# Start order, position table, order of sums at the first gate product, and one spread of a norm in an encoder layer

## The chip, the cores and the metric

The kernel runs on one core of a Trainium2 chip. The metric is the device time of one execution in microseconds; the time before is the median of three runs, 1468.25 us (1464.38 to 1468.91). Five engines work side by side, each through its own queue: TensorE (PE in the profile, its weight loads PEld), VectorE (DVE), ScalarE (ACT), GpSimd (POOL) and SyncE (SP), which here only issues DMAs. DMAs are issued by SyncE, ScalarE and GpSimd.

## The reference

One layer of an encoder for 256 tokens of width 2048 in float32. The parts that matter here:

```python
h = rms_norm(x, attn_norm[i])
proj = h @ w_in[i]
qa, ka, va, qb, kb, vb, ga, gb = jnp.split(proj, split_points, axis=-1)
ya = windowed_gqa(qa, ka, va, rel_bias_table, sink_a[i])
yb = dilated_attention(qb, kb, vb, rel_bias_table)
merged = jax.nn.sigmoid(ga) * (ya @ w_branch_a[i]) + jax.nn.sigmoid(gb) * (yb @ w_branch_b[i])
x = x + merged @ w_out[i]
hf = rms_norm(x, ffn_norm[i])
g = dwconv_centred(hf @ w_ffn_gate[i], conv_w[i], conv_b[i])
x = x + (jax.nn.gelu(g) * (hf @ w_ffn_up[i])) @ w_ffn_down[i]
gate_p = jax.nn.sigmoid(rms_norm(x, ple_norm[i]) @ w_ple_gate[i])
x = x + gate_p * (p[i] @ w_ple_proj[i])
return rms_norm(x, final_norm)
```

Both attentions add a bias to their logits: `table[t5_bucket(rel)]`, a row of a table of 32 buckets by 20 heads, picked by the distance of the two positions.

## The kernel before

**Products.** Every float32 weight is split into two float32r parts, a high one (`whi`, a ScalarE copy, line 261) and a low one (`wlo`, a VectorE subtraction, line 262); activations are split alike (`halves`, `gained`). A product is then taken from three partial products: high by high, high by low, low by high. The weights lie in device memory in the order of use, in pieces of 16 blocks of 128x128; `load` fetches half a piece (512 KB), `split_to` splits it, and `block` and `wide_product` ask for the split three pieces ahead of use. In `block` (lines 324 and 325) the weight is held and 512 columns stream for the high part, 256 for the low one. In `wide_product` (356 to 358) and `seven_product` (400 to 402) the activation is held and 512 weight columns stream. `seven_product` is used for the output and the down projection and forms a 2x2 block product with seven multiplications; its banks are called p1 to p7 and c22.

**Order.** `_plan` writes the list of jobs: first keys, queries and values, then the gates and branch products in quarters, then `o` (output projection, two halves of the columns, n = 0 and 1), then `gg` (the first two gate products together, 32 blocks), then u, g, u, g and so on to the half, `d0`, the second half of the feed-forward beginning with gate product 22 (job `_HALF`), `d1`, then `pp` and `pg`, the embedding part. Work of the other engines is hung into these jobs by `at((job, block), function, ...)`, which `run_due` calls before that block. The program's scheduler may reorder the instructions of an engine; `keep` holds the instructions given to it in program order among themselves.

**Start.** ScalarE issues the norm's columns `cl` (8 KB) and then the first 128 KB chunk of x; SyncE issues the weights and the other chunks of x in the order of the list `order`. TensorE runs `WARM` products of ones in the meantime (line 213). The first seven products share the moving chunks of x (`hs`, lines 454 and 455) and run block by block as they come; 16 chunks are needed, and the first 16 weight blocks form piece 0. The next half piece is the ninth transfer that SyncE issues.

**Position table.** `oh` (which bucket each distance falls into, 32x512) and `tb` (32x20) are loaded on SyncE after all x; one float32 product (line 584) picks the biases, a mask is added (586), and they go to device memory, from where `bias` reads them back.

**The first gate product.** The output projection ends with `joined`, which adds the banks p2, p3, p4 and c22 to the residual rows (line 905) and squares each sum for the second norm (`squares_of`, line 856). (p2, t=0) and (p4, t=1) form one block of 512 columns, (p3, t=0) and (c22, t=1) the next. `flip` turns two column chunks with eight transposes (866) and scales and splits them by `gained` (454 and 455) into `hf`, the moving operand of the gate products; four flips of the last half run inside `gg`, whose blocks 16 to 31 read them. `rms` hangs in the norm: `ask` sums the squares (468), takes the root (474 on VectorE, 476 on GpSimd) and scales the identity into two diagonals `rdg` (484); `tell` spreads them over all partitions by a product with ones (490) and copies the result (501) into `rt[1]`, which the gate's follow-up `after` multiplies in (768).

Of the kernel before, what the change touches and what calls it, by code (L numbers as in the profile page):

```python
# [10 lines left out]
F32 = mybir.dt.float32  # L11
FR = mybir.dt.float32r
AF = mybir.ActivationFunctionType
ALU = mybir.AluOpType
AX = mybir.AxisListType

P = 128
T = 256
D = 2048
# [8 lines left out]
NH = QH + BH  # L28
NBUCK = 32
# [4 lines left out]
EPS = 1e-6  # L34
# [100 lines left out]
FIRST = 7  # L135
START = FIRST + 1
_JOBS = _plan()
WARM = 9
_HALF = next(i for i, j in enumerate(_JOBS) if j[0] == "g" and j[1] == FHALF)


# [48 lines left out]
def _encoder(ctx: ExitStack, tc, xt, pt, cols, table, onehot, mask, ident_in, last_gain, wts, xrows, out):  # L190
    nc = tc.nc
# [7 lines left out]

    x = const.tile([P, KC, T], F32, name="x")  # L200
    cl = const.tile([P, 4 * KC + 4 * FC + QH], F32, name="cl")
    nc.scalar.dma_start(cl[:, :KC], cols[:, :KC])
    nc.scalar.dma_start(x[:, 0:1, :], xt[:, 0:1, :])
    ident = const.tile([P, P], F32, name="ident")
    ones = const.tile([P, P], F32, name="ones")
    nc.vector.memset(ones, 1.0)
# [16 lines left out]
    keep = tc.keep_in_program_order  # L223
# [5 lines left out]
    held = {}  # L229
# [203 lines left out]
    sc = ctx.enter_context(tc.tile_pool(name="sc", bufs=2))  # L433
# [31 lines left out]
    def rowsums(parts):  # L465

        s = sc.tile([P, 2], F32, name="sum")
        nc.vector.tensor_reduce(s, parts, axis=AX.X, op=ALU.add)
        return s

    def root(s, n):

        v = sc.tile([P, n], F32, name="rv", bufs=3)
        nc.vector.tensor_scalar(v, s, 1.0 / D, EPS, op0=ALU.mult, op1=ALU.add)
        r = sc.tile([P, n], F32, name="rr", bufs=3)
        nc.gpsimd.tensor_tensor(r, v, mhalf[:, :n], op=ALU.pow)
        return r

    def norm(s, n):

        r = root(s, n)
        dg = sc.tile([P, T], F32, name="rdg", bufs=1)
        for t in range(2):
            nc.vector.tensor_scalar(dg[:, t * P:(t + 1) * P], ident, r[:, t:t + 1], None, op0=ALU.mult)
        return r, dg

    def spread(dg):
# [5 lines left out]
    def rms(i, total, key, n):  # L493

        def ask():
            rc[key], dg = norm(total(), n)

            def tell():
                b = spread(dg)
                rt[key] = sc.tile([P, T], F32, name="rms")  # L500
                nc.scalar.activation(rt[key], b, AF.Copy)
            for e in i[1:]:
                at(e, tell)
        at(i[0], ask)
# [4 lines left out]
    def at(i, f, *a):  # L509

        due.setdefault(i, []).append((f, a))
# [7 lines left out]
    ap_ = att.enter_context(tc.tile_pool(name="att", bufs=2))  # L519
# [5 lines left out]
    hb1 = big.tile([P, GRP * AW + BH * BW], F32, name="hb1", tag="b1", bufs=1)  # L525
    hba = [hb0, hb1[:, :GRP * AW].rearrange("p (h n) -> p h n", h=GRP)]
    hbb = hb1[:, GRP * AW:].rearrange("p (h n) -> p h n", h=BH)
    oh = ap_.tile([NBUCK, 2 * T], F32, name="oh", tag="near", bufs=2)
    tb = sc.tile([NBUCK, NH], F32, name="tb", bufs=1)
    mk = ap_.tile([NH, 2 * T], F32, name="mk", tag="s1", bufs=2)  # L530

    order = [(0, 1), (0, 0, 1), (0, 1, 3), (0, 3, SUB), (1, 2), (0, SUB, 12), (0, 12, PIECE), (2, 3)]
    chunk = 3
    for r in range(1, FIRST):
        need = -(-((r + 1) * PIECE) // FIRST)
# [3 lines left out]
    for step in order:  # L539
        if len(step) == 3:  # L540
            load(*step)
        elif step[0]:
            nc.sync.dma_start(x[:, step[0]:step[1], :], xt[:, step[0]:step[1], :])
    nc.sync.dma_start(cl[:, KC:], cols[:, KC:])
    nc.sync.dma_start(ident, ident_in)
    nc.sync.dma_start(oh, onehot)
    nc.sync.dma_start(tb, table)
    nc.sync.dma_start(mk, mask)

# [12 lines left out]
    for step in order:  # L562
# [6 lines left out]
        while state["at"] < min(FIRST * ready, _SUBS[state["sub"]][0]):  # L569
            k, e = divmod(state["at"], FIRST)  # L570
# [9 lines left out]
    split_to(state["sub"] + 2)  # L580


    b = ps.tile([NH, 2 * T], F32, name="misc")
    nc.tensor.matmul(b, tb, oh, start=True, stop=True)
    rows = ap_.tile([NH, 2 * T], F32, name="rows", tag="s1", bufs=2)
    keep(nc.vector.tensor_tensor(rows, b, mk, op=ALU.add))
    hold = dram.tile([NH, 2 * T], F32, name="hold")
# [266 lines left out]
    def squares_of(n, t, parts):  # L854
        r = res[:, t, n * W4:(n + 1) * W4]
        keep(nc.scalar.activation(row(), r, AF.Square, accum_out=parts[:, t, n:n + 1]))
# [45 lines left out]
    def joined(n, t, acc, parts):  # L902

        r = res[:, t, n * W4:(n + 1) * W4]
        nc.vector.tensor_tensor(r, acc, r, op=ALU.add)
        squares_of(n, t, parts)

    def gate(n, t, acc, last):

# [48 lines left out]
    for i, job in enumerate(_JOBS):  # L958
# [44 lines left out]
                nc.scalar.dma_start(pr[k], pt[:, k, :])  # L1003
            at((i + 1, 18), layered, pr)
        if kind == "gg":
            rms([(i, 26), (i + 1, 2), (_HALF, 9)], lambda: rowsums(held["ss1"]), 1, 2)
        if kind in ("ga", "gb"):
            at((i, 6), fetch, int(kind == "gb"), n)
        if kind == "bb":
# [2 lines left out]
        if kind == "o":  # L1012
            if n:
                at((i, 11), features)
            for e, k in enumerate((8, 10, 12, 14) if n else (12, 12, 14, 14)):
                at((i + 1, k), flip, 8 * n + 2 * e, "hf", 1)
        if kind == "d1":
            for e, j in enumerate([(i + 2, 0), (i + 2, 0), (i + 3, 1), (i + 3, 1)] if n else
# [41 lines left out]
        if i == FIRST:  # L1060
            for e in range(FIRST):
                late = max(e - KVH, 0)
                at((START + late, 5 if late else 13), after, _JOBS[e], START, None, firsts[e])
            at((START, 13), after, job, START, acc)
        elif kind == "gg":
            for e in range(2):
                at((i + 1, 4 + 4 * e), after, ("g", e), i, acc[e])
        elif kind in ("ga", "gb", "ba", "bb"):
            if kind == "ga":
                if n < QUARTERS - 1:  # L1070
                    th = ap_.tile([P, 2, 2, W4], F32, name="th", tag="v", bufs=1)
                    held["th", n] = {"ga": [th[:, 0, t] for t in range(2)], "gb": [th[:, 1, t] for t in range(2)]}
                else:
                    th = ap_.tile([P, 2, W4], F32, name="th", tag="s3", bufs=1)
                    held["th", n] = {"ga": [th[:, t] for t in range(2)],
                                     "gb": [ap_.tile([P, W4], F32, name="th", tag="s1", bufs=2) for t in range(2)]}
            if kind == "ba":
                held["m"] = ap_.tile([P, 2, W4], F32, name="m", tag="vf", bufs=1)
            for t in range(2):
                if t:  # L1080
                    rest()
                gated(kind, n, t, acc[t])
        elif kind in ("o", "d0", "d1"):
            parts = held["ss1" if kind == "o" else "ss2"]
            for name, t, c in (("p2", 0, 0), ("p3", 0, 1), ("p4", 1, 0), ("c22", 1, 1)):
                if end:
                    joined(2 * n + c, t, acc[name], parts)
                else:
                    a = row()
                    nc.scalar.activation(a, acc[name], AF.Copy)  # L1090
                    to_residual(n, t, c, a)
                    if kind != "d0":
                        at((i + 1, 10), squares_of, c, t, parts)
        elif kind == "pg":
            for t in range(2):
                if t:
                    rest()
                tail = gate(n, t, acc[t], last)
                if last:
                    finish(t, tail)  # L1100
            if n == QUARTERS - 2:
                so_far()
        else:
            after(job, i, acc)
# [49 lines left out]
```

## Time and profile before

| | |
|---|---|
| time, median of three runs | 1468.25 us (1464.38 to 1468.91) |
| profiled execution: span from first to last instruction | 1463.2 us |
| median less span: what lies around it | 5.05 us |
| HBM read, written | 324.06 MB, 27.30 MB |
| cost of all float32 weight splits, ScalarE and VectorE (lines 261, 262; 556 of each) | 564.2 and 650.7 us |
| most frequent DMA: 512 KB of weights, 477 of them, issue to landing | 5.0 us, median |

The profile is one execution on the chip. The profiled execution's own time outside its span is not recorded; the table sets its span beside the median. A line such as L262 is a line of the kernel. In the timeline a row gives start, length, engine, instruction, its output and inputs, and in brackets the engine's idle time before it and what ended it. Matmuls overlap in the pipeline, so the distance from one start to the next says more of them than the length shown.

### The profile page before, as it was taken

To read this page: it belongs to the slowest core of one execution; us is meant where nothing else is said; L and a number is where in the kernel's file an instruction comes from. 1 tells how busy PE (TensorE), PEld (TensorE's weight loads), DVE (VectorE), ACT (ScalarE), POOL (GpSimd) and SP (SyncE) were. 2 spreads that over 40 slices of the span, in tenths; PEclk is the share of its full clock that TensorE was granted. 3 is DMA by queue.
4 is the path that set the end of the run, shared out by engine and by line. 5 is a ranking of instruction groups with operands and counts; after the bars stand their busy time and mean duration, and the time that the engine had idled before them with its cause. 6 is when DMAs were issued, how large, how long until landed. Compare 5 with 4: busy or idle time off the path is not lost.

```text
span 1463.2 us, 20802 instructions
## 1 busy us (share of the span) xinstructions
PE 1449.4 (99%) x7507; PEld 1234.3 (84%) x7507; DVE 1137.2 (78%) x1653; ACT 832.9 (57%) x1196; POOL 107.3 (7%) x178
## 2 busy tenths in 40 slices
PE   9999999999999999999999999999999999999997
PEld 8888888888888888888888888888888888788886
DVE  7687665665665668889998989897999987988665
ACT  7465444444444456665566655675656555666654
POOL 0000000001111100201111100102110100010000
PEclk9999999999999999999999999999999999999999
DMA  9754555557888967978788786989878864797652
GB/s 322 245 177 159 172 170 171 188 178 262 286 314 294 354 229 254 296 237 283 269 293 270 273 284 212 285 287 304 279 273 282 289 244 159 266 294 249 217 193 89
DMA packets 111731, 362.17 MB, mean 248 GB/s; under 512 B 12804, under 2 KB 17924, under 8 KB 111500
## 3 DMA queue, kind: packets, MB, share of 16 engines
q1 hardware_dynamic: 88908, 292.80, 57.5%
q0 software_dynamic: 20560, 63.71, 14.4%
q10 hardware_dynamic: 2160, 4.33, 0.9%
q8 instruction: 59, 0.97, 0.3%
q14 instruction: 44, 0.36, 0.1%
HBM read 324.06 MB, written 27.30 MB: 240 GB/s over the span
## 4 chain that ended last, share of the span: by engine, by line
PE 96%; DVE 1%; issue 1%; DMA 1%; ACT 0%; POOL 0%; POOLq 0%; DVEq 0%; ACTq 0%
PE acc L324 28%; PE acc L325 14%; PE acc L356 9%; PE acc L358 9%; PE acc L357 9%; PE acc L401 7%; PE acc L400 7%; PE acc L402 7%; PE first L324 2%; PE first L325 1%; PE pt L669 1%; DMA raw<-in_wts 0%; PE pt L866 0%; DVE wlo L262 0%; PE sp L628 0%
## 5 line engine op out<-in xcount | busy, mean ns | idle before, releaser
L262 DVE TENSOR_TENSOR wlo<-raw,whi 128x1024 fp32r<-128x1024 f32 (+2 forms) x556 | 650.7, 1181 | 264.3 <-ACT whi L261 258.9
L261 ACT ACTIVATE whi<-raw 128x1024 fp32r<-128x1024 f32 (+2 forms) x556 | 564.2, 1025 | 473.5 <-PE acc L358 188.7
L324 PE MATMUL acc<-mov,whi 128*128 128x512 f32 x1840 | 642.2, 395 | 0.3 <-DVE mov L455 0.3
L325 PE MATMUL acc<-mov,wlo 128*128 128x256 f32 x1840 | 511.0, 278 | 0.0
L324 PEld LDWEIGHTS acc<-mov,whi 128*128 128x128 f32 x1840 | 345.0, 188 | 79.5 <-DVE mov L455 0.6
L325 PEld LDWEIGHTS acc<-mov,wlo 128*128 128x128 f32 x1840 | 346.0, 188 | 0.5
L356 PE MATMUL acc<-whi,mov 128*128 128x512 f32 (+1 forms) x512 | 196.5, 384 | 0.0
L358 PE MATMUL acc<-whi,mov 128*128 128x512 f32 (+1 forms) x512 | 196.3, 383 | 0.0
L357 PE MATMUL acc<-wlo,mov 128*128 128x512 f32 (+1 forms) x512 | 196.2, 383 | 0.0
L356 PEld LDWEIGHTS acc<-whi,mov 128*128 128x128 f32 x512 | 96.7, 189 | 19.3 <-DVE first L444 0.8
L358 PEld LDWEIGHTS acc<-whi,mov 128*128 128x128 f32 x512 | 96.6, 189 | 18.8
L357 PEld LDWEIGHTS acc<-wlo,mov 128*128 128x128 f32 x512 | 96.6, 189 | 18.4
L400 PE MATMUL acc<-whi,act 128*128 128x512 f32 x207 | 80.9, 392 | 0.2 <-ACT whi L261 0.2
L401 PE MATMUL acc<-wlo,act 128*128 128x512 f32 x207 | 80.9, 391 | 0.0
L402 PE MATMUL acc<-whi,act 128*128 128x512 f32 x207 | 80.6, 389 | 0.0
L825 POOL DMA_DIRECT2D x<-row x36 | 31.1, 879 | 380.0 <-ACT row L830 258.1
L262 DVE TENSOR_TENSOR wlo<-sums,whi 128x1024 fp32r<-128x1024 f32 x37 | 45.1, 1219 | 9.9 <-ACT whi L261 9.9
L400 PEld LDWEIGHTS acc<-whi,act 128*128 128x128 f32 x207 | 38.8, 188 | 9.5 <-ACT whi L261 1.5
L401 PEld LDWEIGHTS acc<-wlo,act 128*128 128x128 f32 x207 | 38.9, 188 | 8.9 <-DVE wlo L262 0.9
L401 PE MATMUL acc<-wlo,shl 128*128 128x512 f32 x116 | 45.6, 393 | 0.0
L402 PEld LDWEIGHTS acc<-whi,act 128*128 128x128 f32 x207 | 38.9, 188 | 8.0
L402 PE MATMUL acc<-whi,shl 128*128 128x512 f32 x116 | 45.2, 390 | 0.0
(203 smaller groups left out, 1669.5 us busy)
## 6 DMA issues: line engine op xcount, KB each, us to landing
raw<-in_wts SPq DMA_DIRECT2D x477, 512.0 KB, 5.0
sums<-kept SPq DMA_DIRECT2D x37, 512.0 KB, 5.6
sums<-in_wts POOLq DMA_DIRECT2D x23, 512.0 KB, 6.8
kept<-sums POOLq DMA_DIRECT2D x23, 512.0 KB, 4.1
raw<-in_wts SPq DMA_DIRECT2D x39, 256.0 KB, 4.9
row<-in_wts POOLq DMA_DIRECT2D x37, 256.0 KB, 8.2
x<-row POOLq DMA_DIRECT2D x36, 256.0 KB, 7.7
two<-in_wts POOLq DMA_DIRECT2D x14, 512.0 KB, 8.0
```

What stands on the lines that cost most here:

```text
L261: nc.scalar.activation(hi, src, AF.Copy)
L262: ins = nc.vector.tensor_tensor(lo, src, hi.bitcast(F32), op=ALU.subtract)
L324: nc.tensor.matmul(acc, hi[:, o, :], m, start=first, stop=False, skip_group_check=True)
L325: nc.tensor.matmul(acc[:, T:], lo[:, o, :], m[:, :T], start=False, stop=last, skip_group_check=True)
L356: nc.tensor.matmul(acc, xh, hi, start=(k == 0), stop=False)
L357: nc.tensor.matmul(acc, xh, lo, start=False, stop=False)
L358: nc.tensor.matmul(acc, xl, hi, start=False, stop=(k == n - 1))
L400: nc.tensor.matmul(acc, xh, hi, start=(e == 1), stop=False)
L401: nc.tensor.matmul(acc, xh, lo, start=False, stop=False)
L402: nc.tensor.matmul(acc, xl, hi, start=False, stop=(e == uses[name]))
L669: nc.tensor.transpose(p[:, k, t * P:(t + 1) * P], s[:, t, (c + k) * P:(c + k + 1) * P], ident)
L825: keep(nc.gpsimd.dma_start(quarter(n, t, c), a, accum_op=ALU.add))
```

## The change

It has five parts. (1) ScalarE issues the first chunk of x first, then the columns, then chunks 1 and 2 of x in one transfer, which leave SyncE's queue; one warm-up product less. (2) The position table is split into two float32r halves, on ScalarE and VectorE, and multiplied in two float32r products; `oh` becomes float32r and is loaded by GpSimd. (3) In `joined` the additions come in the order p2, p4, p3, c22 and are kept in program order; for the output projection the squares are moved to blocks 18, 20, 22 and 24 of the job behind. The last half's first two flips move from blocks 8 and 10 to 6 and 8. (4) The second norm is asked for at block 28 of `gg` instead of 26 and spread at block 7 of the next job instead of block 2, and the two gate follow-ups move from blocks 4 and 8 to 8 and 12; the VectorE part of root and diagonals is kept in program order. (5) The spread of the same norm at block 9 of the second half's first gate product is left out.

```diff
-WARM = 9
+WARM = 8
...
+    nc.scalar.dma_start(x[:, 0:1, :], xt[:, 0:1, :])
     nc.scalar.dma_start(cl[:, :KC], cols[:, :KC])
-    nc.scalar.dma_start(x[:, 0:1, :], xt[:, 0:1, :])
+    nc.scalar.dma_start(x[:, 1:3, :], xt[:, 1:3, :])
...
-        nc.vector.tensor_scalar(v, s, 1.0 / D, EPS, op0=ALU.mult, op1=ALU.add)
+        keep(nc.vector.tensor_scalar(v, s, 1.0 / D, EPS, op0=ALU.mult, op1=ALU.add))
...
-            nc.vector.tensor_scalar(dg[:, t * P:(t + 1) * P], ident, r[:, t:t + 1], None, op0=ALU.mult)
+            keep(nc.vector.tensor_scalar(dg[:, t * P:(t + 1) * P], ident, r[:, t:t + 1], None, op0=ALU.mult))
...
-    oh = ap_.tile([NBUCK, 2 * T], F32, name="oh", tag="near", bufs=2)
+    oh = ap_.tile([NBUCK, 2 * T], FR, name="oh", tag="near", bufs=2)
     tb = sc.tile([NBUCK, NH], F32, name="tb", bufs=1)
+    tbs = sc.tile([NBUCK, 2, NH], FR, name="tbs", bufs=1)
...
+    by_scalar = 3
...
-        elif step[0]:
+        elif step[0] >= by_scalar:
             nc.sync.dma_start(x[:, step[0]:step[1], :], xt[:, step[0]:step[1], :])
...
-    nc.sync.dma_start(oh, onehot)
+    nc.gpsimd.dma_start(oh, onehot)
...
+    nc.scalar.activation(tbs[:, 0], tb, AF.Copy)
+    nc.vector.tensor_tensor(tbs[:, 1], tb, tbs[:, 0].bitcast(F32), op=ALU.subtract)
     b = ps.tile([NH, 2 * T], F32, name="misc")
-    nc.tensor.matmul(b, tb, oh, start=True, stop=True)
+    for e in range(2):
+        nc.tensor.matmul(b, tbs[:, e], oh, start=(e == 0), stop=(e == 1))
...
-        nc.vector.tensor_tensor(r, acc, r, op=ALU.add)
-        squares_of(n, t, parts)
+        keep(nc.vector.tensor_tensor(r, acc, r, op=ALU.add))
...
-            rms([(i, 26), (i + 1, 2), (_HALF, 9)], lambda: rowsums(held["ss1"]), 1, 2)
+            rms([(i, 28), (i + 1, 7)], lambda: rowsums(held["ss1"]), 1, 2)
...
-            for e, k in enumerate((8, 10, 12, 14) if n else (12, 12, 14, 14)):
+            for e, k in enumerate((6, 8, 12, 14) if n else (12, 12, 14, 14)):
...
-                at((i + 1, 4 + 4 * e), after, ("g", e), i, acc[e])
+                at((i + 1, 8 + 4 * e), after, ("g", e), i, acc[e])
...
-            for name, t, c in (("p2", 0, 0), ("p3", 0, 1), ("p4", 1, 0), ("c22", 1, 1)):
+            for e, (name, t, c) in enumerate((("p2", 0, 0), ("p4", 1, 0), ("p3", 0, 1), ("c22", 1, 1))):
                 if end:
                     joined(2 * n + c, t, acc[name], parts)
+                    if kind == "o":
+                        at((i + 1, 18 + 2 * e), squares_of, 2 * n + c, t, parts)
+                    else:
+                        squares_of(2 * n + c, t, parts)
```

## The prediction

> **What bounds the kernel now.** I read the page first, for the busy shares:
>
> ```profile
> span 1463.2 us, 20802 instructions
> PE 1449.4 (99%) x7507; PEld 1234.3 (84%) x7507; DVE 1137.2 (78%) x1653; ACT 832.9 (57%) x1196; POOL 107.3 (7%) x178
> ```
>
> TensorE stands still for 1463.2 - 1449.4 = 13.8 us in all. So an edit can pay in two ways only: by taking work off PE, or by closing one of its few gaps. The view by stages says where the gaps are (columns: stretch, its length, busy PE, PEld, DVE, ACT, POOL, granted clock, DMA share, GB/s):
>
> ```profile
> 0.00:6.00 6.00, 4.44 (x19) 4.14 (x20) 1.23 (x5) 2.97 (x6) 0.20 (x4) 1.00 0.59 184
> 6.00:45.00 39.00, 38.40 (x221) 33.31 (x221) 30.21 (x39) 27.25 (x39) 0.00 (x0) 1.00 0.92 327
> 590.00:660.00 70.00, 68.88 (x344) 57.05 (x343) 58.87 (x85) 47.69 (x79) 9.71 (x13) 1.00 0.84 261
> 660.00:890.00 230.00, 230.00 (x1321) 200.87 (x1320) 205.58 (x363) 135.66 (x215) 23.82 (x44) 1.00 0.78 269
> 1330.00:1463.00 133.00, 123.59 (x562) 102.29 (x560) 85.10 (x106) 71.03 (x102) 3.52 (x5) 0.97 0.54 181
> ```
>
> The last row's 9.4 us is the final norm and the output, which the change leaves alone. The rest, about 4 us, lies in the first 12 us, around the first gate product (590 to 660), and at one place shown further down. The view of waits, for PE, names what ended them:
>
> ```profile
> PE pt L866 <- DVE mov L455: 0.6, 1, 0.6
> PE first L324 <- ACT whi L261: 0.6, 1, 0.6
> PE misc L490 <- ACT row L1090: 0.6, 1, 0.6
> PE first L324 <- DVE mov L455: 0.5, 1, 0.5
> PE acc L324 <- DVE mov L455: 0.3, 1, 0.3
> ```
>
> All five lie where the change works. The runs' median is 1468.25 us, 5.05 us over the profiled span; I make the sum against the span and add those 5.05.
>
> **The start.** The timeline of the first microseconds (start, length, instruction, and the idle time before it with what ended it), then two steps of the chain of waits (start, length, what):
>
> ```profile
> 1.06 4.21 PE L213 MATMUL misc<-ones 128*128 128x128 f32 x18 [1.06 <-DVE mhalf L208]
> 1.19 0.45 ACTq L203 DMA_DIRECT2D x<-in_xt  x1
> 2.13 0.43 SPq L543 DMA_DIRECT2D x<-in_xt  x1
> 3.55 0.93 SPq L543 DMA_DIRECT2D x<-in_xt  x2
> 4.69 0.51 ACT L454 ACTIVATE mov<-x,cl 128x256 fp32r<-128x256 f32 x1 [1.32 <-DMA x<-in_xt]
> 5.77 0.50 PE L324 MATMUL first<-mov,whi 128*128 128x512 f32 x1 [0.51 <-DVE mov L455]
> 11.33 0.28 PE L325 MATMUL first<-mov,wlo 128*128 128x256 f32 x1
> ```
>
> ```profile
> 4.62 6.38 DMA raw<-in_wts
> 12.21 1.66 PE first L324 x6
> ```
>
> Today the first chunk of x is issued on ScalarE at 1.19, behind the columns, whose issue I take to be as long as its own, 0.45 us; ScalarE's wait for it ends at 4.69, and the first product runs at 5.77. With x issued first everything up to there may come 0.45 us earlier. The columns then follow x in the same queue and are needed by the same scaling (L454), so the gain can be less. The ninth warm-up product (4.21 / 9 = 0.47 us) goes; PE waits afterwards anyway, so that is worth nothing by itself, and it merely keeps the warm-up out of the earlier first product's way. ScalarE's third issue pushes its first work back by some 0.45 us; the 1.32 us it waits for x covers that.
>
> The point is the second gap. PE starts its 16th block's last product at 11.33 and stands until 12.21, for the split of a weight piece that was issued at 4.62 and landed at 11.00. Whatever is won at 5.77 is lost here unless that piece lands earlier. The change takes two issues of x from ahead of it on SyncE (0.43 at 2.13 and one of the pair at 3.55), so it is issued about 0.86 us sooner. Its landing took 6.38 us for 512 KB, though at the 327 GB/s of the second row these bytes alone need 1.6: it queues behind bytes, and the bytes ahead are the same ones. The onehot table (64 KB) moves from SyncE at 26 us to the idle POOL and may now start in the first microseconds, 64 KB / 327 GB/s = 0.2 us against us. So the end moves by between -0.2 (all bytes, table ahead) and +0.86 us (all issue time). With a DMA share of 0.92 I stay near the byte end: **0.2 us**. The second chunk's scaling was ready 0.7 us ahead of its use; that it now comes as part of 256 KB on ScalarE's queue can open a small gap at 8 us, which the gap at 11.33 swallows.
>
> The Trainium skill (DMA: Bandwidth & Descriptors, Issuing engines are not separate DMA queues) says that DMAs started from several engines run on the same 16 engines and interleave, and that spreading them saves only sequencer time. By it the start would gain the issue time at most, and nothing where bytes are the limit, which is how the 6.38 us reads.
>
> **The table.** Rows around 45 us, and the nearest rows for the new small instructions:
>
> ```profile
> 45.55 0.28 PE L325 MATMUL first<-mov,wlo 128*128 128x256 f32 x1
> 45.76 1.03 PE L584 MATMUL misc<-oh,tb 32*20 32x512 f32 x2
> 46.72 0.39 PE L356 MATMUL acc<-whi,mov 128*128 128x256 f32 x1
> 44.06 1.23 DVE L262 TENSOR_TENSOR wlo<-raw,whi 128x1024 fp32r<-128x1024 f32 x1 [1.55 <-ACT whi L261]
> 48.09 1.20 DVE L262 TENSOR_TENSOR wlo<-raw,whi 128x1024 fp32r<-128x1024 f32 x1
> 27.43 0.32 SPq L547 DMA_DIRECT2D tb<-in_table  x1
> 2.96 0.21 ACT L210 ACTIVATE warm<-mhalf 128x4 f32<-128x4 f32 x1
> ```
>
> The float32 product is two instructions; from the end of the last block (45.55 plus 0.12 for 256 columns) to the next product at 46.72 it costs 1.05 us. Two float32r products of 512 columns take 0.23 each, by the step from L324 to L325 further down (994.08 to 994.31), with the 0.1 before 45.76 that is 0.56: **0.5 us** saved. Bounds: 0, if 32 rows in float32r cost as much as now, and 0.6. The two halves of the table cost one small ScalarE instruction (at least 0.21) and one small VectorE subtraction (no more than the 1.23 of a weight's), and both have from the table's landing until 45.7: it is issued at 27.43, and even the 512 KB piece above landed within 6.4 us. If that cover is gone because they are queued late, PE waits for them; this is the rival below.
>
> **The first gate product.** VectorE, ScalarE and PE between 638 and 646:
>
> ```profile
> 640.27 0.15 DVE L468 TENSOR_REDUCE sum<-marks 128x2 f32<-128x8 f32 x1
> 641.47 0.48 DVE L484 TENSOR_SCALAR rdg<-ident,rr 128x128 f32<-128x128 f32 x2 [0.84 <-POOL rr L476]
> 643.00 0.87 DVE L455 SCALAR_TENSOR_TENSOR mov<-pt,cl,mov 128x256 fp32r<-128x256 f32 x2
> 639.30 0.62 ACT L856 ACTIVATE row<-x 128x512 f32<-128x512 f32 x1
> 642.94 0.28 PE L325 MATMUL acc<-mov,wlo 128*128 128x256 f32 x1
> 643.54 0.50 PE L324 MATMUL acc<-mov,whi 128*128 128x512 f32 x1 [0.31 <-DVE mov L455]
> 644.66 1.06 PE L866 MATMUL pt<-ident,x 128*128 128x128 f32 x8 [0.62 <-DVE mov L455]
> ```
>
> PE loses 643.54 - (642.94 + 0.12) = 0.48 and 644.66 - (643.54 + 0.35) = 0.77: 1.25 us, both to the low halves of the turned features (L455). What held those up: the norm was asked for at block 26, and VectorE's queue had it first. From 640.27 to the end of the diagonals (641.47 + 0.48) that is 1.7 us, 0.84 of it waiting for POOL's root. And ScalarE ran four squares (0.62 us each, the last at 639.30) ahead of the high halves. The change puts the squares at blocks 18 to 24, the norm at 28, the additions of both token halves of one column block (p2 and p4) first, since a turn reads both, and the first two turns two blocks (0.7 us) sooner. VectorE is then free for the low halves from 640.27: 640.3 to 641.15 for the first turn's pair instead of 643.00 to 643.87, to 642.0 for the second's. The first wait is gone. For the second, turns at blocks 12 and 14 need the banks that these two pairs free; PE comes to them at 642.94 - 0.23 - 3 x 0.35 = 641.7 and, two blocks and a turn later, 642.7. Gone too, by half a microsecond. I take **1.1** of 1.25; bounds -0.5 and 1.25. What is late next is the norm itself: its spread moves to block 7 of the up product, some 651.6, while sums, root and diagonals end near 650.5. If they end a microsecond later PE waits 0.5 there, the lower bound. The gate's follow-up starts 1.4 us later in a stretch where DVE is 205.58 of 230 us busy and PE never waits; the weights are split three pieces of 2.8 us ahead, which hides it. No squares, turns or sums are added. Squares and sums of the down product keep their times; there only the order of two additions differs, in a stage where PE has no gap.
>
> **The spread left out.** Before 1000 us:
>
> ```profile
> 994.08 0.39 PE L324 MATMUL acc<-mov,whi 128*128 128x512 f32 x1
> 994.31 0.28 PE L325 MATMUL acc<-mov,wlo 128*128 128x256 f32 x1
> 997.13 0.28 PE L325 MATMUL acc<-mov,wlo 128*128 128x256 f32 x1
> 997.99 0.70 PE L490 MATMUL misc<-rdg,ones 128*128 128x256 f32 x2 [0.57 <-ACT row L1090]
> 998.34 0.58 PE L324 MATMUL acc<-mov,whi 128*128 128x512 f32 x1
> ```
>
> The second half no longer spreads the same norm again. PE passes from 997.13 + 0.12 to 998.34, 1.1 us, of which 0.74 is the wait for the bank that the L1090 copy frees. Nothing else asks for that bank then, and the next gate block's weights are there: **1.1 us**; bounds 0.35 (another wait takes the place) and 1.1.
>
> **Sum:** 0.2 + 0.5 + 1.1 + 1.1 = 2.9 us; span 1460.3, time 1465.3. From the bounds: best 0.9 + 0.6 + 1.25 + 1.1 = 3.9; worst -0.2 + 0 - 0.5 + 0.35, about no change.
>
> **Rivals.**
> (1) Only the work taken off PE counts, the waits come back elsewhere: 0.5 for the table and 0.35 for the spread, 0.9 us, 1467.4. For it: the start's second gap, and the half microsecond at the banks. Against it: the two waits at the gate have named causes that the change moves. 18%.
> (2) The table's halves come late, and it ends **slower**. The subtraction is a new VectorE instruction, and PE waits for it, with the whole values product behind it. If it is queued behind the gathers and the weight split at 48.09, it is done near 49.4 and PE stands from 45.7: 3.7 us, against 2.9 won, 1469.0. It decides from a wait of 2.9 us on. Against it: the table has landed long before, and the split at 44.06 ends by 45.3. 8%.
> (3) The PE clock. The warm-up's 18 instructions of 128 columns took 4.21 us, 0.234 each, while the spread's 256 columns at 997.99 pass in 0.35 / 2 = 0.175: the warm-up ran at well under full rate, and the first 16 blocks already step by (11.33 - 5.77) / 16 = 0.35. If eight are too few and the slow rate lasts as long again as PE had worked before its first product (5.77 - 1.06 = 4.7 us), half of it, 2.35 us, is lost, less the 0.88 of the second gap: 1.5 net, 1466.8. 6%. The Trainium skill (TensorE: Matmul & The Clock Gate, Part 1) has the clock at half until a window of about 3.4 us was busy, windows running freely; the slow warm-up agrees, and an estimate from that figure, half of one more window, is 1.7 us lost before the gap.
> (4) Every bound at its best: 3.9 us, 1464.4. 8%.
>
> **From cases to numbers.** My forecast, 1465.3, has 60%. What is told apart here is about 0.3%, 4.4 us: the three runs of one program already span 1464.38 to 1468.91. All listed gains together do not reach 4.4, so faster needs case (4) or the forecast with luck in the medians: 0.14. Slower by 4.4 us needs (2) at more than twice its price, or a wait I do not see: 0.06. Within: 0.80. The range takes (4) less about 3 us of what runs differ by, and (2) with a little: 1461.3 to 1469.4.
>
> **What would show it.** The start: first product near 5.3 and the gap before the 17th block ending at 12.0. The table: two L584 successors, 0.23 apart, with no wait before them. The gate: no PE wait on L455 between 638 and 646, and L490 in the up product without one. One L490 pair less, and PE unbroken at 997. I am wrong if PE's idle time comes back at another row, above all before the table or at L490, or if the weight pieces land later at the start.

## The result, and the profile after

The changed kernel is slower. Its median is 1473.32 us (1472.07 to 1475.00, ten runs) beside 1467.57 us of the kernel before (1464.38 to 1471.74, ten runs): ratio 1.0035, interval 1.0023 to 1.0046. The forecast was 1465.3 us, with a range up to 1469.4.

The first lines of the page of the changed kernel:

```profile
span 1471.4 us, 20796 instructions
PE 1456.6 (99%) x7503; PEld 1237.3 (84%) x7503; DVE 1136.7 (77%) x1654; ACT 834.1 (57%) x1196; POOL 108.1 (7%) x179
```

The span grew by 8.2 us and PE's busy time by 7.2, though PE runs four instructions fewer. So most of the loss is not waiting. The products themselves take longer. The granted clock is the same (0.998 in both). The profiled execution of the changed kernel took 1473.2 us, 1.8 us more than its span, and the same 1.8 separates time and span in the other runs; the profiled execution of the kernel before was therefore one of about 1465.0, not of the median 1468.25.

The waits of PE in the changed kernel (total, times, longest) and the stages that the prediction showed of before:

```profile
PE first L325 <- ACT whi L262: 1.3, 1, 1.3
PE pt L872 <- PE acc L403: 1.0, 1, 1.0
PE first L325 <- DVE mov L456: 0.7, 1, 0.7
PE acc L325 <- DVE mov L456: 0.4, 1, 0.4
```

```profile
0.00:6.00 6.00, 4.21 (x21) 4.01 (x22) 1.20 (x5) 2.50 (x5) 0.89 (x5) 1.00 0.61 170
6.00:45.00 39.00, 37.49 (x211) 31.71 (x210) 29.09 (x38) 26.90 (x38) 0.00 (x0) 1.00 0.88 320
590.00:660.00 70.00, 68.33 (x335) 56.42 (x334) 56.81 (x76) 47.00 (x76) 10.65 (x13) 1.00 0.85 262
660.00:890.00 230.00, 230.00 (x1327) 202.71 (x1327) 207.24 (x368) 137.17 (x220) 23.87 (x44) 1.00 0.78 270
1330.00:1471.00 141.00, 131.55 (x590) 107.56 (x589) 91.75 (x113) 75.84 (x108) 3.58 (x5) 0.98 0.56 182
```

PE now stands for 1.5 us between 6 and 45 us (before 0.6) and for 1.7 us around the gate product (before 1.1). The end is unchanged (141.0 - 131.55 = 9.45 us). The wait at L490 in the second half is gone, as it should be. What PE stands still for has grown by some 1 us in all (8.2 - 7.2), and 8.2 are to be explained.

So I compared the two traces by stage: how late PE reaches the same point of its work, as the difference of start times (us, after minus before; in the last column what the stage itself added; each figure is rounded by itself).

```
point of PE's work                     before    after   later by   stage added
end of the first seven products          45.5     47.0     +1.4        +1.4
first sums (behind the table)            60.5     61.5     +1.0        -0.4
last turn of the branch products        557.0    560.7     +3.7        +2.7
end of the output projection            636.4    640.8     +4.5        +0.8
start of the first down product         884.3    888.8     +4.4         0.0
its end                                 993.9   1000.7     +6.8        +2.4
start of the second down product       1239.5   1244.9     +5.5        -1.3
its end                                1353.4   1361.2     +7.7        +2.2
span                                   1463.2   1471.4     +8.2        +0.5
```

Not all of the 1.4 us at the top is the start's: from the 31st to the 111th block of the first seven products, without a wait, the changed kernel takes 353 ns a block and the kernel before 347, which makes 0.5 us.

7.3 of the 8.2 us (2.7 + 2.4 + 2.2) arise in the attention and branch products and in the two down products, which the change doesn't touch. The groups of instructions there, first of the kernel before, then of the changed one (busy us, mean ns of one):

```profile
L400 PE MATMUL acc<-whi,act 128*128 128x512 f32 x207 | 80.9, 392 | 0.2 <-ACT whi L261 0.2
L401 PE MATMUL acc<-wlo,act 128*128 128x512 f32 x207 | 80.9, 391 | 0.0
```

```profile
L402 PE MATMUL acc<-wlo,act 128*128 128x512 f32 x207 | 82.3, 397 | 0.0
L401 PE MATMUL acc<-whi,act 128*128 128x512 f32 x207 | 81.8, 397 | 0.2 <-ACT whi L262 0.2
```

The same 207 products show 5 to 6 ns more each. Since the lengths overlap, the timeline of PE in the changed kernel says it better, where the values' products end (held `mov`) and the first branch products begin (held `yab`):

```profile
353.53 0.39 PE L358 MATMUL acc<-wlo,mov 128*128 128x512 f32 x1
353.76 0.39 PE L359 MATMUL acc<-whi,mov 128*128 128x512 f32 x1
353.98 0.39 PE L357 MATMUL acc<-whi,mov 128*128 128x512 f32 x1
354.21 0.39 PE L358 MATMUL acc<-wlo,mov 128*128 128x512 f32 x1
354.44 0.40 PE L359 MATMUL acc<-whi,mov 128*128 128x512 f32 x1
354.67 0.39 PE L357 MATMUL acc<-whi,yab 128*128 128x512 f32 x1
354.90 0.40 PE L358 MATMUL acc<-wlo,yab 128*128 128x512 f32 x1
355.14 0.39 PE L359 MATMUL acc<-whi,yab 128*128 128x512 f32 x1
355.37 0.39 PE L357 MATMUL acc<-whi,yab 128*128 128x512 f32 x1
```

No wait, the same shapes, the same line of code: with `mov` held four steps take 353.53 to 354.44, 0.2275 us each; with `yab` held three take 354.67 to 355.37, 0.233 each. Five nanoseconds are the size that is looked for: 621 products hold `act`, 348 its sums `shl` (both in the down products) and 288 `yab`, and the steps of these 1257 together rose by 6.3 us. Of the 2.7 us in the attention and branch products they explain 1.9; the other 0.7 or so lies ahead of the first branch product and was not broken down.

### The profile page after: what moved, and what is told of

Read it like the earlier page. It is cut to its first block, busy times and chain, and to the rows that moved or that the text cites. A ratio compares the mean times of both kernels' runs of the same rounds, so it can differ in the third digit from the quotient of the medians.

```text
span 1471.4 us, 20796 instructions
## 1 busy us (share of the span) xinstructions
PE 1456.6 (99%) x7503; PEld 1237.3 (84%) x7503; DVE 1136.7 (77%) x1654; ACT 834.1 (57%) x1196; POOL 108.1 (7%) x179
## 4 chain that ended last, share of the span: by engine, by line
PE 92%; issue 6%; POOL 1%; DMA 0%; ACT 0%; DVE 0%; SPq 0%; POOLq 0%; DVEq 0%; ACTq 0%
PE acc L325 28%; PE acc L326 15%; PE acc L358 9%; PE acc L357 9%; PE acc L359 9%; PE acc L402 5%; PE acc L401 5%; PE acc L403 5%; PE first L325 1%; PE first L326 1%; PE pt L675 0%; POOL x L831 0%; DMA raw<-in_wts 0%; PE pt L872 0%; PE misc L690 0%
## 5 line engine op out<-in xcount | busy, mean ns | idle before, releaser
L403 PE MATMUL acc<-whi,act 128*128 128x512 f32 x207 | 81.3, 393 | 0.0
L403 PEld LDWEIGHTS acc<-whi,act 128*128 128x128 f32 x207 | 38.9, 188 | 9.1
```

The costliest lines, as they stand in the source:

```text
L403: nc.tensor.matmul(acc, xl, hi, start=False, stop=(e == uses[name]))
```

## The experiments

**The theories.** Place (A): the new tile `tbs` takes 2 x 20 x 4 = 160 bytes of each partition, and every tile that the program's allocation puts behind it moves by 160 bytes, `yab` and `act` among them; `whi`, `wlo` and `mov` stay where they were, and so does `shl`, which takes over the two slots of `merged` in the pool `big`. By the addresses that the programs give their tiles, all of these operands begin at byte 160 modulo 256 in the kernel before; in the changed kernel `act` and `yab` begin at 64. The products step slower when the held operand no longer begins at the same byte, within some power of two, as the streamed one. Its rival (B): the loss lies in the change's own order, its waits and transfers. A third, the cadence (C), was added when the first runs showed it: the long rows of gate and up products run in one of two steady beats, and what stands ahead of them chooses. Medians are in us; before is measured beside each on the same chip.

**Make the tile 256 bytes (e1).** In the changed kernel:

```diff
-    tbs = sc.tile([NBUCK, 2, NH], FR, name="tbs", bufs=1)
+    tbs = sc.tile([NBUCK, 2, 32], FR, name="tbs", bufs=1)
```

with `tbs[:, e, :NH]` where it is used.

> The changed kernel with its new table tile made 256 instead of 160 bytes long per partition, so that every tile allocated behind it starts 256 instead of 160 bytes later than before the change. Theory A, the place of the tiles: the products whose held operand lies in yab or act step by 0.227 us again (whi and wlo by act, 0.231 to 0.238 in the changed kernel), their sum falls by about 6.3 us, and the time is about 1467 (1473.3 less 6.3). Rival B, the new order and the new waits cost the time: steps stay at 0.231 to 0.238 and the time at 1473.

Measured: 1470.73 (1469.27 to 1474.90), ratio 1.0028 (1.0016 to 1.0040). By the medians, each set against the kernel before on its own chip, 1.6 of the 6.3 us came back (5.75 over it, now 4.13). By stages all of the place did: attention and branches added -0.1 instead of +2.7 (behind the first sums), the first down product 0.0 instead of +2.4, the second 0.1 instead of +2.2. In its stead the second half of the feed-forward now took 3.4 us longer than before, where the changed kernel had been 1.3 shorter. PE in the same place as above:

```profile
353.90 0.39 PE L359 MATMUL acc<-whi,mov 128*128 128x512 f32 x1
354.12 0.39 PE L357 MATMUL acc<-whi,yab 128*128 128x512 f32 x1
354.35 0.39 PE L358 MATMUL acc<-wlo,yab 128*128 128x512 f32 x1
354.58 0.39 PE L359 MATMUL acc<-whi,yab 128*128 128x512 f32 x1
```

The step stays at 0.227 across the change of the held operand.

**Shift alone, in the kernel before (e2, e4).** Nothing of the change, only a longer table tile, by 160 and by 128 bytes (56 columns):

```diff
-    tb = sc.tile([NBUCK, NH], F32, name="tb", bufs=1)
+    tb = sc.tile([NBUCK, 60], F32, name="tb", bufs=1)[:, :NH]
```

> The kernel before with nothing but its table tile made 160 bytes longer per partition: no instruction is added, moved or removed, only the tiles behind it start 160 bytes later. Theory A: wlo by act steps by 0.237 instead of 0.227, and the kernel is about 6 us slower than before, some 1474. Rival B: the same time as before, 1467.6, and steps of 0.227.

> The kernel before with its table tile 128 bytes longer per partition. Under theory A this tells the rule of the step: if the distance of the held operand's start to the streamed one's counts modulo 64 or 128 bytes, wlo by act steps by 0.227 as before and the span is that of before; if modulo 256 bytes or more, it steps by 0.232 to 0.238. Rival B: 0.227.

Measured: e2 1481.35 (1475.93 to 1482.98), ratio 1.0098 (1.0077 to 1.0118); e4, a single run, 1474.0. Forty floats of padding, never read, cost more than the whole change, and 7 us more than theory A expected. e2's six runs fall into two groups, two at 1475.9 and 1476.5 and four at 1481.3 to 1483.0; the profile is one of the lower group, so the 5 us between the groups are not traced. The steps from one product to the next (median ns, and the sum of the group in us) say why:

```
held, streamed   x    before      changed     e1 (256)    e2 (160)    e4 (128)
act, whi        414   227  94.8   231  96.6   227  94.9   231  96.5   232  97.2
act, wlo        207   227  47.4   237  48.8   227  47.3   237  48.9   232  48.2
shl, whi        232   227  53.5   232  54.1   227  53.4   232  54.2   230  53.7
shl, wlo        116   227  26.8   236  27.4   227  26.8   236  27.4   227  26.9
yab, whi        192   227  43.6   231  44.5   227  43.6   231  44.6   232  44.7
yab, wlo         96   227  21.8   238  22.8   227  21.8   237  22.7   232  22.3
merged, wlo      88   227  20.0   226  20.0   226  20.0   227  20.0   227  20.0
```

A shift by 256 bytes changes nothing, shifts by 160 and 128 do, and `merged`, which doesn't move, keeps its step. That is the place of `act` and `yab`, shown from both sides; their share of the 6.3 us is 5.1. The other 1.2 are `shl`'s, which lies at the same addresses in all five kernels. Its products alternate with those of `act` in the down products; why they slow down with them is not shown. But the profile of e2 lost another 4.5 us between the output projection and the first down product. PE's groups there (660 to 880 us), first of the kernel before, then of e2:

```profile
L324 PE MATMUL acc<-mov,whi 128*128 128x512 f32 x636 | 220.5, 394 | 0.0
L325 PE MATMUL acc<-mov,wlo 128*128 128x256 f32 x635 | 175.9, 277 | 0.0
```

```profile
L324 PE MATMUL acc<-mov,whi 128*128 128x512 f32 x624 | 220.5, 399 | 0.0
L325 PE MATMUL acc<-mov,wlo 128*128 128x256 f32 x623 | 175.1, 281 | 0.0
```

In the same 220 us PE passes 12 blocks fewer without ever waiting: 346.7 ns for a block in the one, 353.3 in the other. Neither operand of these products had moved. This is the second cause, C.

**The old start (e3) and the new start alone (e8).** e3 is e1 with the order of transfers of before and nine warm-up products; e8 is the kernel before with the new order:

```diff
+    nc.scalar.dma_start(x[:, 0:1, :], xt[:, 0:1, :])
     nc.scalar.dma_start(cl[:, :KC], cols[:, :KC])
-    nc.scalar.dma_start(x[:, 0:1, :], xt[:, 0:1, :])
+    nc.scalar.dma_start(x[:, 1:3, :], xt[:, 1:3, :])
```

> The first kernel of this set with the start put back: columns first, then the first chunk of x on ScalarE, chunks 1 and 2 on SyncE, nine warm-up products. In the changed kernel the first seven products end 1.4 us later than before (46.95 against 45.55), with a wait of 1.3 us for the third split at 7.8. If the new order of issue makes that, they end at 45.6 again and this kernel is 1.4 us faster than the first of the set, some 1465.5; if the onehot table, which is still issued by GpSimd at the front, makes it, they end near 46.9 here too and the two times agree.

> The kernel before with the new start alone: x first, then the columns, then chunks 1 and 2 on ScalarE, eight warm-up products; the onehot table stays on SyncE. If the new order of issue costs the 1.4 us at the first seven products, their last product starts near 47 and the third split is waited for at about 7; if the table issued early by GpSimd does, the last product starts at 45.5 or sooner (kernels with the old start: 44.9 to 45.8).

Measured: e3 1469.71 (1468.34 to 1471.03), 1.0 us below e1; e8, a single run, 1470.73, with the slow beat (see below) in its second half, so its time says nothing of the start. Over all profiles, the first seven products end at 46.2 to 47.5 us in the five with the new start (mean 46.8) and at 44.9 to 46.7 in the ten with the old one (mean 46.0). These ranges overlap, so a single profile decides nothing here, but both readings, the medians of e1 and e3 and the means of the profiles, make the new start 0.8 to 1.0 us worse. Where it goes, in the changed kernel and then in e3:

```profile
1.67 0.45 ACTq L204 DMA_DIRECT2D x<-in_xt  x1
...
4.03 0.51 ACT L455 ACTIVATE mov<-x,cl 128x256 fp32r<-128x256 f32 x1 [0.37 <-DMA cl<-in_cols]
5.20 0.47 PE L325 MATMUL first<-mov,whi 128*128 128x512 f32 x1 [0.73 <-DVE mov L456]
7.01 0.74 ACT L262 ACTIVATE whi<-raw 128x640 fp32r<-128x640 f32 x1 [1.97 <-DMA raw<-in_wts]
7.80 0.74 PE L325 MATMUL first<-mov,whi 128*128 128x512 f32 x2 [1.32 <-ACT whi L262]
```

```profile
5.86 0.74 ACT L261 ACTIVATE whi<-raw 128x640 fp32r<-128x640 f32 x1 [0.18 <-DMA raw<-in_wts]
```

The first product starts at 5.20, 0.6 us sooner than before. But ScalarE's next split, the third, then stands 1.97 us for its weights, until 7.01, where e3 has them at 5.86, and PE waits 1.32 us for it. The late split holds everywhere: it starts at 6.83 to 7.09 in all five profiles with the new start, and at 5.53 to 6.01 in all ten with the old one. e8, with the bucket table still on SyncE, is among the late (6.83), and e3, with the early table, among the early, so the order of issue makes it and not the table. The early first product does not hold: 5.20 is the soonest of the five, which start at 5.8 in the mean, the ten at 5.6.

A second loss appears in two of the five. The timeline of PE in k4 (the changed kernel with two later edits, see below), and the row of stages of e1 from 8 to 11 us, columns as in the prediction, with the granted clock at 0.50:

```profile
9.22 0.63 PE L325 MATMUL first<-mov,whi 128*128 128x512 f32 x1
...
9.86 0.63 PE L325 MATMUL first<-mov,whi 128*128 128x512 f32 x1
...
10.93 0.39 PE L325 MATMUL first<-mov,whi 128*128 128x512 f32 x1
...
11.27 0.39 PE L325 MATMUL first<-mov,whi 128*128 128x512 f32 x1
```

```profile
8.00:11.00 3.00, 3.00 (x10) 2.21 (x10) 2.65 (x6) 2.40 (x6) 0.00 (x0) 0.50 1.04 405
```

In k4 a block takes 0.64 us, and from 10.9 on 0.34. PE runs there at about half its later rate, from 5.8 to 10.5 us, and e1 does so from 8.1 to 11.3, which costs some 2.3 and 1.6 us. The longest such stretch behind the first product in the other profiles is 1.4 us (k1). The row of e1 has the clock at 0.50; the same view gives 1.00 for k4 from 6 to 10 us, so it does not always show this. Both kernels have eight warm-up products, but so have three profiles without it; whether the missing ninth brings it about was not tried.

**The spread and the beat (e5, e6, e7).** e5 is e1 with the third spread put back; e6 is the kernel before without it; e7 is e6 with a small float32 product of ones in its place, whose result is used nowhere.

```diff
-            rms([(i, 26), (i + 1, 2), (_HALF, 9)], lambda: rowsums(held["ss1"]), 1, 2)
+            rms([(i, 26), (i + 1, 2)], lambda: rowsums(held["ss1"]), 1, 2)
```

> The changed kernel with 256 bytes for the table tile and, besides, the third spread put back at block 9 of the second half's first gate product. Theory C, the cadence: in the profile of the 256-byte kernel every block of the second half's gate and up products took 353.3 ns, in that of before 346.7 ns, and in before the blocks ahead of the spread still took 353; the wait at the spread sets PE's cadence anew. Then the blocks behind the spread take 346.7 ns, the second half gains 4.5 us and pays 1.1 for the spread, and the time is about 1467.3. Rival D, the cadence is drawn anew in each run and the spread has no part in it: the time is 1.1 us over that of the 256-byte kernel, 1471.8.

> The kernel before with the third spread left out and nothing else. Theory C: the second half keeps the cadence of 353.3 ns that the down product leaves behind, 4.5 us lost against 1.1 saved, some 1470 against 1466.6. Rival D and the prediction: 1.1 us faster, 1465.5, blocks of 346.7 ns as often as before.

> The kernel before with the third spread replaced by one product of ones, 128 columns, into a free bank at the same block: it breaks the row of blocks but waits for nothing. Theory C in its wide form, any break sets the cadence anew: blocks of 346.7 ns behind it and about 1 us faster than before, 1465.6. In its narrow form, only a wait does: 353.3 ns and some 1470. Rival D: 1465.6 on the whole, blocks of either length.

Measured: e5 1467.62 (1466.15 to 1472.74), ratio 1.0003 (0.9991 to 1.0015); e6 1468.92 (1468.05 to 1470.07), 1.0008 (0.9997 to 1.0018); e7 1469.39 (1468.03 to 1470.78), 1.0010 (1.0000 to 1.0020). Taking 1.1 us of PE out of the kernel before does not make it faster, and putting it back doesn't make e1 slower. e5's median is theory C's 1467.3, but by seven of its twelve runs only, and its one profile has 353.3 ns behind the spread, as rival D allowed. PE's groups between 1000 and 1235 us, of the kernel before and of e6:

```profile
L324 PE MATMUL acc<-mov,whi 128*128 128x512 f32 x679 | 235.4, 393 | 0.0
L325 PE MATMUL acc<-mov,wlo 128*128 128x256 f32 x679 | 188.1, 277 | 0.0
```

```profile
L324 PE MATMUL acc<-mov,whi 128*128 128x512 f32 x667 | 235.7, 399 | 0.0
L325 PE MATMUL acc<-mov,wlo 128*128 128x256 f32 x666 | 187.0, 281 | 0.0
```

12 blocks fewer in 235 us, 353.3 ns each instead of 346.7. In the kernel before, too, the second half begins in the slow beat, at 994, and the wait and spread at 997.99 end it. Without them it lasts to the end of the half: 686 blocks by 6.6 ns are 4.5 us, against the 1.1 that are saved, and e6's second half took 3.4 us longer.

The times show the same. With the spread the kernel before falls into two groups on one chip, 19 of its 29 runs between 1464.5 and 1467.9 and 10 between 1469.5 and 1471.9 (on two other chips the gap between the groups is less clear); e5 does too, seven and five, and its profiled run, of the upper group, has the slow beat in the second half; so has e8's, at 1470.73. e6, and the changed kernel, have one group each. So after a wait the beat seems to fall differently from run to run, and without one it is fixed by the program. No two profiles of one kernel, one of each group, were taken; that the upper group is the slow beat is argued from e5, e8 and the size of the gap.

The beat in which the second half begins goes with the place of `act`. Right behind the first down product, ahead of any wait, the blocks take about 347 ns in the three kernels whose `act` lies 160 or 128 bytes further (changed, e2, e4) and 353 in the twelve other profiles. So the shift that made the two down products 4.6 us longer seems also to have given the changed kernel the fast beat that e1 and e6 lack; no run moved `act` alone.

**A product that sets the beat (k1 to k4).** k1 and k2 are the kernel before with the table in float32r halves (a tile of 256 bytes), without the third spread, and with the product of ones at block 10 and 11. k3 has a float32r product of 256 columns at block 9 instead; its result is used nowhere. k4 is e1 with the same product.

```diff
+    def pulse():
+        b = ps.tile([P, T], F32, name="pulse", tag="sp", bufs=2)
+        m = held["hf"][:, 0, :]
+        nc.tensor.matmul(b, m[:, :P], m[:, :T], start=True, stop=True)
...
-            rms([(i, 26), (i + 1, 2), (_HALF, 9)], lambda: rowsums(held["ss1"]), 1, 2)
+            at((_HALF, 9), pulse)
+            rms([(i, 26), (i + 1, 2)], lambda: rowsums(held["ss1"]), 1, 2)
```

> A kernel made from what has held: before, with the position table in two float32r halves (the onehot still on SyncE and converted by VectorE, the table tile 256 bytes), the third spread left out, and one product of 128 columns of ones at block 10 of the second half's first gate product, where block 9 did not change the cadence. If a break without a wait can change it at another place in the three-block pattern, the second half's blocks take 346.7 ns and the span is some 1461.5 (before's fast profile 1463.2 less 0.4 and 1.1); if never, 353.3 ns and some 1466.

> The same with the product at block 11, the third place of the pattern: 346.7 ns and a span of some 1461.5, or 353.3 ns and some 1466.

> The same with one float32r product of 256 columns at block 9 instead, which lasts differently than the two passes of float32: 346.7 ns and a span of some 1461.5, or 353.3 ns and some 1466. If all three of this set stay at 353.3, only a wait sets the cadence.

Measured, a single run each: k1 1470.16 and k2 1468.90, both with 353.3 ns a block in the second half; k3 1464.83, with 346.7. The timeline of PE around the product, in the timed run of k3:

```profile
996.75 0.40 PE L324 MATMUL acc<-mov,whi 128*128 128x512 f32 x1
...
997.81 0.28 PE L863 MATMUL pulse<-mov 128*128 128x256 f32 x1
997.93 0.40 PE L324 MATMUL acc<-mov,whi 128*128 128x512 f32 x1
...
998.98 0.39 PE L324 MATMUL acc<-mov,whi 128*128 128x512 f32 x1
...
1000.01 0.40 PE L324 MATMUL acc<-mov,whi 128*128 128x512 f32 x1
```

Three blocks take 996.75 to 997.81, 1.06 us, ahead of the product, and 997.93 to 998.98 and 998.98 to 1000.01, 1.05 and 1.03, behind it (three times 353.3 ns are 1.060 us, three times 346.7 are 1.040). Nothing waits on either side. Timed:

> The kernel with the float32r product of 256 columns at block 9, timed. If the cadence behind a product without a wait is fixed by the instructions, every execution lies within some 2 us and none in a second group 4 us higher, as before's do (10 of 29 above 1469): about 1465, against 1466.8. If it is drawn in each run, a third of the executions lie near 1469.

> The changed kernel as it is, but with 256 bytes for the table tile and the same float32r product of 256 columns at block 9 of the second half's first gate product. If place and cadence are all that the change cost beyond its start, this removes both: 1470.7 (256 bytes) less 4.5, some 1466.3, executions in one group, start still 1 us late. If something else of the change costs time too, it stays above 1467.5.

Measured: k3 1464.00 (1462.88 to 1464.56, twelve runs) beside 1465.80 of before, ratio 0.9982 (0.9971 to 0.9994): faster than both kernels, and in one group. k4 1466.40 (1464.79 to 1468.18, without a clear gap), ratio 0.9995 (0.9984 to 1.0007). So the changed kernel with its tile at 256 bytes and one product that sets the beat is level with the kernel before; its profile ends 0.2 us later, with the first seven products 1.9 us late, the half rate shown above among them, and 2.1 made up again: 0.4 by the table, 1.1 in the second half without the spread, 0.6 in the output projection. Another 0.4 is lost behind the second down product.

## Why the prediction was wrong

**The step that failed** stands in its second paragraph: "So an edit can pay in two ways only: by taking work off PE, or by closing one of its few gaps." It took the time from one product to the next as a property of the instruction, and the table's halves as costing "one small ScalarE instruction ... and one small VectorE subtraction". They also cost 160 bytes, and by them 6.3 of the 8.2 us in the three groups with `act`, `shl` and `yab`, far from the table (5.1 in the two that moved). No rival had it, and none was as dear: the worst sum was "about no change", and the price of rival (2) 3.7 us. The code holds a hint: `yab` is cut from element 40, 160 bytes in, of a longer tile.

**Around the span.** The 5.05 us between median and span were carried as a constant. They were 1.8 us, and 3.2 by which the profiled execution was quicker than the median. The time was to be set against the two groups of the kernel before, which three runs (1468.25, 1464.38, 1468.91) already hinted at.

**The start** had the right places and the wrong sign: forecast 0.2 us won, bounds -0.2 and 0.86; lost 1.4 in this profile, 0.5 of it by the beat, and 0.8 to 1.0 by all. That the first product came at 5.20 (forecast 5.3) is luck: with the same start it came at 5.69 to 6.34 in four other profiles. The gap at 11.33 that was to swallow a small gap at 8 closed, and the one at 8 grew to 1.3. The prediction looked at issue times of the transfers that moved to ScalarE and not at the weights behind them: 256 KB of x issued at 1.67 run beside weight pieces that are needed sooner. One of its signs of being wrong, weight pieces that land later at the start, came true. The Trainium skill's sentence on issuing engines (DMA: Bandwidth & Descriptors, Issuing engines are not separate DMA queues) agrees, if the rows 7.01 and 5.86 are read as the price of the interleaving; it was cited as bounding the gain only, not as a loss.

**The table** was right, 0.4 us for 0.5:

```profile
46.95 0.28 PE L326 MATMUL first<-mov,wlo 128*128 128x256 f32 x1
47.16 0.62 PE L590 MATMUL misc<-oh,tbs 32*20 32x512 f32 x2
47.71 0.39 PE L357 MATMUL acc<-whi,mov 128*128 128x256 f32 x1
```

From 46.95 + 0.12 to 47.71 are 0.64 us where there were 1.05. Rival (2), late halves, did not come: PE doesn't wait here. Rival (3), a PE that is late at its full rate, did not come in this profile, whose products step by 232 ns from 5.62 us on. It did in those of e1 and k4, at some 1.6 and 2.3 us; the prediction had 2.35 ahead of the gap. The stages from 0 to 6 us have the clock at 1.00 in all of these kernels and do not tell them apart.

**The first gate product**: forecast 1.1 us, measured nothing. From the end of the output projection to the down product PE took 247.95 us before, 247.93 now, and 247.95 and 247.90 in e1 and k4. The view of waits has 0.6 us there (0.2 + 0.4) where it had 0.9, but the stage is no shorter. The waits moved, as rival (1) had it:

```profile
649.85 0.16 DVE L469 TENSOR_REDUCE sum<-marks 128x2 f32<-128x8 f32 x1
651.06 0.48 DVE L485 TENSOR_SCALAR rdg<-ident,rr 128x128 f32<-128x128 f32 x2 [0.84 <-POOL rr L477]
651.46 1.22 DVE L263 TENSOR_TENSOR wlo<-raw,whi 128x1024 fp32r<-128x1024 f32 x1
652.60 0.87 DVE L456 SCALAR_TENSOR_TENSOR mov<-pt,cl,mov 128x256 fp32r<-128x256 f32 x2
653.13 0.50 PE L325 MATMUL acc<-mov,whi 128*128 128x512 f32 x1 [0.43 <-DVE mov L456]
```

The norm, its wait for POOL's root and now a weight split too stand ahead of the low halves of the last turn (652.60), and PE waits for these. The prediction moved the first two turns out of the norm's way and let the last one run into it. The output projection added 0.8 us in this profile, with a wait of 1.0 (L872 behind L403). That stage varies from profile to profile, 0.6 us shorter than before in k4 and 1.5 longer in k1, whose output projection is that of before; I don't count it as an effect of the change.

**The spread left out** was right where it stands (the second half is 1.3 us shorter, forecast 1.1) and would have been wrong in a kernel with its tiles in place: in e1 and e6 the same edit costs 3.4 us or so by the beat. The changed kernel was spared that because it began the second half in the fast beat, which goes with the displaced `act`, so the agreement is in part luck. The prediction asked whether another wait takes the place. It did not ask what the wait did for the products behind it.

**What stays open.** Why the first half has the slow beat in e2 and e4 and the fast one elsewhere, and why one product sets the beat and another (e7, k1, k2) doesn't. Why the beat behind the down product goes with `act`'s place, and why `shl`, which doesn't move, slows down with it. Whether the place counts relative to the streamed operand or by itself: `whi` and `wlo` were never moved. The start's loss was not divided between the late third split and the stretches at half rate, and what brings these about was not tried.

## What to carry to other kernels

When a change adds or resizes a tile, look up which operands of the main products move, and try its size rounded up to 256 bytes before anything else is judged. Where one engine is busy 99% of the time, compare first its steps for groups that the change doesn't touch, then its waits; a removed wait may have been what set the beat of the work behind it. When the runs of one kernel fall into groups, compare group with group, and stage by stage, because two effects of the same size and opposite sign hide in one median (e1).

## What the runs showed of the hardware

Float32r products of 512 columns with the operand held at 128x128 step by 227 ns when the held and the streamed tile begin at the same byte within 256, and by 231 to 238 ns with the held one (`act`, `yab`) 160 or 128 bytes further; a shift by 256 gave 227 again. Products with `shl` held, which did not move but alternate with those of `act`, stepped by 232 to 236 ns at 160 bytes and by 227 to 230 at 128. Pairs of 512 and 256 columns run for over 200 us without a wait at either 346.7 or 353.3 ns a pair, at a granted clock of 1.00 in both. What stands ahead of them decides which: one odd product in k3 and k4, a wait (not always the same way), or, in the profiles at hand, the place of the operand held in the products ahead. In the first microseconds PE can run at half rate after it has begun its work: 426 and 214 ns for 512 and 256 columns up to 10.5 us in k4, and from 8.1 to 11.3 in e1, against 230 and 117 behind it. The Trainium skill (TensorE: Matmul & The Clock Gate, the section "Wait — 56ns, not 53.3ns?") gives the step by the number of columns alone, 215.7 ns for 512 when the clock is up. The groups in the table of steps above take 227 to 238 ns, and these decide.
